# Issuing the job loads and stores of a float32 decoder layer in four parts of 256 KB

## The chip, the cores and the metric

The kernel runs on one core of one Trainium2 chip. The metric is the time of one execution on the device, in microseconds (us). The core has TensorE (PE in the profile; its weight loads are PEld), VectorE (DVE), ScalarE (ACT), GpSimd (POOL) and SyncE (SP). SP, ACT and POOL can issue DMA transfers, which are carried out by the core's 16 DMA engines. Transfers that SP issues appear as queue q1 in the profile, transfers that POOL issues as queue q0. An engine executes its instructions in a fixed order; an instruction that has to wait for a semaphore holds up everything behind it on the same engine.

## The reference

One decoder layer on 256 tokens with 2048 features, all in float32:

```
x = x + concat(pool_mixer, mla_mixer, memory_cross_attention)(rms_norm(x) @ w_in) @ w_o
h = rms_norm(x)
g = h @ w_gate                                  # 2048 x 5632
gc = conv_b + sum_j conv_w[j] * shift(g, j)     # causal, width 3
x = x + (silu(gc) * (h @ w_up)) @ w_down        # 5632 x 2048
```

The last three lines are the feed-forward block, and the change lies in its weights of `w_down`.

## The kernel before, in words

**Splitting.** TensorE multiplies rounded float32 (float32r), so each weight tile is split in two: `split_w` (lines 96 to 105) has ScalarE round a block of 1024 columns into `wh` (L102), and VectorE subtract that from the raw tile into `wl` (L103). A product is then three matmuls. In the gate and up stage `gemm_pair` (L155 to L170) does this: for each of 44 tiles f of 128 features of `w_gate` and `w_up`, 96 matmuls at L168.

**The loop over f.** The loads of the two 1 MB weight tiles come from `load_w` on SP's queue (L89), into a buffer `wr` of three; they are pinned in program order. After a step's matmuls, `glu` (L827 on) does the convolution and the gate on VectorE and ScalarE: `g` L829, `gc` L831, L833, L834, and then the product with the up half (L839 or L850). For 17 of the 22 pairs of tiles of f, `glu` also builds seven forms of the activation (L854 to L858); five pairs are written out to DRAM by POOL (L860, `forms`).

**Seven products in place of eight.** Down's weights are seen as 2 x 2 blocks of 512 columns and multiplied by a scheme of Strassen's kind that needs seven products. It needs sums of weight blocks. For 28 pairs of column half and feature pair (`SUMMED`) the sums are made ahead of time, as "jobs" beside the gate and up stage, and are kept in DRAM in `tsum`. A job loads a 1 MB tile of `w_down`, 128 partitions of 8 KB, into one of two buffers `wj` (`job_load`, L873 to L877); VectorE makes four subtractions in place, each on blocks of 512 columns (L883): block 1 from 0 and 1, block 0 from 2 and 0, block 2 from 2 and 1, block 3 from 3 and 2; then POOL stores the tile to `tsum` in two halves of 512 KB (L885). Loads, subtractions and stores are pinned (`keep`) behind what was traced before them on their engine.

**When.** The loads of jobs 0 and 1 come at the head of the loop and after step 1. `job_at` (L887) gives job i the step 1 + 37 i // 27, that is one after one or two steps of f. At that step the kernel first issues the load of job i + 1 and then the subtractions and stores of job i (L907 to L910). POOL thus has load i + 1 ahead of the stores of job i, and load i + 1 goes to the buffer of job i - 1, whose stores must have landed.

**Order.** The Tile framework traces the program, decides the order on each engine by its own simulation with its own instruction costs, and puts in the semaphores. Where `keep` pins an instruction it stays behind its predecessor in the program; the splits of `gemm_pair` are not pinned and are placed by the planner.

**Down.** After the loop, down loads raw tiles and the sums from `tsum` with SP (`load_dn`, L922 to L929), every third of them into a buffer `wj`. SP's queue takes them in the planner's order among the last loads of `w_gate` and `w_up`.

Of the kernel before, what the change touches and what calls it, by code (L numbers as in the profile page):

```python
# [37 lines left out]
HS = 1024  # L38
NN = 512
# [6 lines left out]
SUMMED = tuple((c, j) for c in range(2) for j, k in zip(ORDER, KIND) if k == "S")  # L46
# [18 lines left out]
def layer(ctx, tc, xT_d, xn_d, memT_d, vec_d, tab_d, w_z_d, w_mqkr_d, w_q_d, w_kv_d, w_mem_d, w_pool_d, w_o_d,  # L65
          w_g_d, w_u_d, w_dn_d, out_d):
    nc = tc.nc
# [18 lines left out]
    def load_w(src, n, cut=STG, kept=False):  # L86
        raw = stage.tile([P, STG], F32, tag="wr", name=nm("wr"), bufs=3)
        for c in range(0, n, cut):
            keep(nc.sync.dma_start(raw[:, c:min(n, c + cut)], src[:, c:min(n, c + cut)]), kept)  # L89
        return raw[:]  # L90

    def keep(ins, on=True):

        return tc.keep_in_program_order(ins) if on else ins
# [240 lines left out]
    for c in range(KD // 2):  # L335
        raw = raw0 if c == 0 else load_w(w_mem_d[c], STG, HS if c == 1 else STG)
# [9 lines left out]
        if c % 2:  # L346
            h = slice(2 * c - 2, 2 * c + 2)
# [68 lines left out]
    for c in range(KD // 2):  # L416
        raw = load_w(w_mqkr_d[c], 2 * 576)
# [110 lines left out]
    for m in range(6):  # L528
        raw = load_w(w_z_d[m], STG)
# [338 lines left out]
    tsum = dp.tile([P, len(SUMMED), STG], F32, name="tsum")  # L868

    def job_place():  # L870
        return fp.tile([P, STG], F32, tag="wj", name=nm("wj"), bufs=2)[:]

    def job_load(i):  # L873

        raw = job_place()
        keep(nc.gpsimd.dma_start(raw, w_dn_d[SUMMED[i]]))  # L876
        return i, raw  # L877

    def job_sums(i, raw):

        r = raw.rearrange("p (b n) -> p b n", n=NN)
        for d, a, b in ((1, 0, 1), (0, 2, 0), (2, 2, 1), (3, 3, 2)):
            keep(nc.vector.tensor_tensor(r[:, d], r[:, a], r[:, b], op=ALU.subtract))  # L883
        for h in range(2):
            keep(nc.gpsimd.dma_start(tsum[:, i, h * HS:(h + 1) * HS], raw[:, h * HS:(h + 1) * HS]))  # L885

    job_at = {1 + i * (KF - 7) // (len(SUMMED) - 1): i for i in range(len(SUMMED))}  # L887

# [8 lines left out]
    for ps, raw in zip(pss, raws):  # L897
        gemm_t(ps, raw, HS, h2, range(8, KD), first=False)
    job = job_load(0)
    for f in range(1, KF):  # L900
        rows = [load_w(w[f], STG, kept=True) for w in (w_g_d, w_u_d)]
        behind = (lambda p=pss: glu(0, *p)) if f == 1 else None
        pss = [ps_main()[:, 0:T] for _ in range(2)]
        gemm_pair(pss, rows, h2, behind)
        if f < KF - 1:
            glu(f, *pss)
        if f in job_at:  # L907
            now, n = job, job_at[f] + 1
            job = job_load(n) if n < len(SUMMED) else None
            job_sums(*now)  # L910
# [213 lines left out]
```

## Time and profile before

| what | value |
|---|---|
| time, median of 3 runs (lowest to highest) | 1006.77 us (1006.08 to 1007.03) |
| the profiled execution: its time, its span | 1005.68 us, 1003.9 us |
| TensorE / VectorE / ScalarE / POOL busy | 99% / 78% / 57% / 7% |
| job loads (L876) | 28 of 1024 KB, median 7.4 us from issue to landing |
| job stores (L885) | 56 of 512 KB, median 10.4 us from issue to landing |
| job subtractions (L883) | 112, mean 686 ns |
| the stretch of the jobs | first load at 297.5 us, last store at 733.8 us |

A row of a timeline has the start, the length, the engine and line, the operation, the tiles written and read, and in square brackets the engine's idle time ahead of it with what ended it. A row of a queue has the packets, the megabytes, and the time that they took as a share of 16 engines over the window. The row of a wait has the total, the number of times, and the longest.

### The profile page before, as it was taken

Reading aid. Unit: us, or ns where it says so; the run is one execution under the profiler, and the core shown is the slowest. Engines: PE = TensorE matmul, PEld = TensorE weight load, DVE = VectorE, ACT = ScalarE, POOL = GpSimd, SP = SyncE. Lnnn points to the kernel's source line nnn. Section 1 sums busy time; section 2 is a strip of 40 time slices with the busy share of each in tenths; the row PEclk is TensorE's granted clock in tenths of the full one; section 3 lists DMA queues with packets and bytes.
Section 4 is the critical chain, followed back from the end, with each engine's and each line's share of the span. In section 5 each row is a group of like instructions: output and inputs, shape, how many; then the busy total and the mean of one; then the engine's idle time right before and its main releaser. Section 6 shows DMA issues by size and latency. Waiting matters only on the chain.

```text
span 1003.9 us, 17322 instructions
## 1 busy us (share of the span) xinstructions
PE 992.0 (99%) x6870; PEld 917.6 (91%) x6870; DVE 785.1 (78%) x1174; ACT 570.9 (57%) x779; POOL 66.8 (7%) x130
## 2 busy tenths in 40 slices
PE   9999999999999999999999999999999999999998
PEld 8899988888899999999989999999999888888886
DVE  6877588755667887868868888788667889989987
ACT  6777666544565545435445545545445666757763
POOL 1100000000010110101011101011000000000000
PEclk9999999999999999999989999999999999999999
DMA  9867445333667988888889998999898999999992
GB/s 360 292 247 282 146 143 199 131 133 129 226 223 295 338 302 323 314 326 294 334 301 339 358 331 308 343 359 358 309 350 323 333 372 367 363 342 395 367 385 109
DMA packets 50578, 294.89 MB, mean 294 GB/s; under 512 B 5696, under 2 KB 6208, under 8 KB 25024
## 3 DMA queue, kind: packets, MB, share of 16 engines
q1 hardware_dynamic: 33696, 213.16, 57.3%
q0 software_dynamic: 16368, 79.83, 22.5%
q8 instruction: 54, 0.88, 0.3%
q10 hardware_dynamic: 432, 0.79, 0.2%
q14 instruction: 28, 0.23, 0.1%
HBM read 255.61 MB, written 38.14 MB: 293 GB/s over the span
## 4 chain that ended last, share of the span: by engine, by line
PE 84%; DMA 10%; DVE 4%; issue 1%; ACT 1%; POOL 0%; SPq 0%; DVEq 0%; POOLq 0%; ACTq 0%
PE psm L168 33%; DMA tsum<-wj 6%; PE psm L184 5%; PE psm L185 5%; PE psm L186 5%; PE psm L149 4%; PE psa L935 4%; PE psa L934 4%; PE psm L935 4%; PE psa L933 4%; PE psm L934 4%; PE psm L933 4%; PE psm L133 2%; DMA wr<-in_w_g 2%; DMA wj<-in_w_dn 2%; DVE wl L103 2%
## 5 line engine op out<-in xcount | busy, mean ns | idle before, releaser
L103 DVE TENSOR_TENSOR wl<-wr,wh 128x1024 fp32r<-128x1024 f32 (+2 forms) x344 | 396.7, 1161 | 127.8 <-ACT wh L102 119.3
L102 ACT CAST wh<-wr 128x1024 fp32r<-128x1024 f32 (+2 forms) x344 | 339.8, 1000 | 166.0 <-PE psm L185 49.1
L168 PE MATMUL psm<-h,wh 128*128 128x256 f32 x2752 | 320.9, 277 | 0.6 <-ACT wh L102 0.6
L168 PEld LDWEIGHTS psm<-h,wh 128*128 128x128 f32 x2752 | 316.9, 188 | 0.8 <-ACT wh L102 0.8
L168 PE MATMUL psm<-h,wl 128*128 128x256 f32 x1376 | 167.2, 279 | 5.9 <-DVE wl L103 5.9
L168 PEld LDWEIGHTS psm<-h,wl 128*128 128x128 f32 x1376 | 161.8, 189 | 7.4 <-DVE wl L103 7.3
L831 ACT ACTIVATE gc<-g,vec 128x256 f32<-128x256 f32 x44 | 26.5, 602 | 111.9 <-DVE g L829 111.0
L883 DVE TENSOR_TENSOR wj<-wj 128x512 f32<-128x512 f32 x112 | 76.8, 686 | 15.1 <-DMA wj<-in_w_dn 14.0
L102 ACT CAST wh<-wj 128x1024 fp32r<-128x1024 f32 (+1 forms) x48 | 47.2, 982 | 22.0 <-PE psa L934 11.6
L103 DVE TENSOR_TENSOR wl<-wj,wh 128x1024 fp32r<-128x1024 f32 (+1 forms) x48 | 53.7, 1132 | 6.0 <-ACT wh L102 2.4
L834 ACT ACTIVATE gc<-gc 128x256 f32<-128x256 f32 x44 | 18.4, 418 | 57.2 <-DVE gc L833 57.2
L833 DVE SCALAR_TENSOR_TENSOR gc<-g,vec,gc 128x255 f32<-128x255 f32 x88 | 42.2, 480 | 1.5
L103 DVE TENSOR_TENSOR wl<-dn,wh 128x1024 fp32r<-128x1024 f32 (+1 forms) x36 | 40.1, 1132 | 3.4 <-ACT wh L102 1.7
L102 ACT CAST wh<-dn 128x1024 fp32r<-128x1024 f32 (+1 forms) x36 | 35.4, 982 | 10.7 <-PE psm L934 4.9
L184 PE MATMUL psm<-wh,cat 128*128 128x512 f32 x96 | 38.1, 397 | 0.0
L186 PE MATMUL psm<-wl,cat 128*128 128x512 f32 x96 | 37.4, 390 | 0.0
L185 PE MATMUL psm<-wh,cat 128*128 128x512 f32 x96 | 37.4, 389 | 0.0
L885 POOL DMA_DIRECT2D tsum<-wj x56 | 29.8, 534 | 86.8 <-DVE wj L883 69.8
L876 POOL DMA_DIRECT2D wj<-in_w_dn x28 | 15.0, 536 | 282.3 <-DMA tsum<-wj 274.8
L934 PE MATMUL psm<-wh,aS 128*128 128x512 f32 x84 | 32.7, 389 | 0.0
L933 PE MATMUL psa<-wh,aS 128*128 128x512 f32 x84 | 32.7, 389 | 0.0
L933 PE MATMUL psm<-wh,aS 128*128 128x512 f32 x84 | 32.7, 389 | 0.0
(248 smaller groups left out, 1473.5 us busy)
## 6 DMA issues: line engine op xcount, KB each, us to landing
wr<-in_w_g SPq DMA_DIRECT2D x44, 1024.0 KB, 7.9
wr<-in_w_u SPq DMA_DIRECT2D x44, 1024.0 KB, 7.7
wj<-in_w_dn POOLq DMA_DIRECT2D x28, 1024.0 KB, 7.4
tsum<-wj POOLq DMA_DIRECT2D x56, 512.0 KB, 10.4
wr<-in_w_o SPq DMA_DIRECT2D x16, 1024.0 KB, 4.8
wr<-in_w_dn SPq DMA_DIRECT2D x16, 768.0 KB, 6.9
wr<-tsum SPq DMA_DIRECT2D x12, 1024.0 KB, 6.8
wj<-tsum SPq DMA_DIRECT2D x12, 1024.0 KB, 7.2
```

Source lines behind the costliest of these rows:

```text
L102: keep(nc.scalar.copy(hi[:, c:e], raw[:, o + c:o + e]), kept)
L103: keep(nc.vector.tensor_tensor(lo[:, c:e], raw[:, o + c:o + e], hi[:, c:e].bitcast(F32), op=ALU.subtract), kept)
L149: keep(nc.tensor.matmul(ps, parts[k // nk][low][:, i * P:(i + 1) * P], m, start=k + a == 0 and low == low_first, stop=k == KD - 1 and low ...
L168: nc.tensor.matmul(ps, parts[k // nk][low][:, i * P:(i + 1) * P], m, start=k + a == 0 and low == (s == 1), stop=k == KD - 1 and low == (s ...
L184: keep(nc.tensor.matmul(ps, xh, hi[:, i, o], start=first and i == 0, stop=False), kept)
L185: keep(nc.tensor.matmul(ps, xl, hi[:, i, o], start=False, stop=False), kept)
L186: keep(nc.tensor.matmul(ps, xh, lo[:, i, o], start=False, stop=last and i == nk - 1), kept)
L833: nc.vector.scalar_tensor_tensor(gc[:, d:T], g[:, 0:T - d], v(w, f), gc[:, d:T], op0=ALU.mult, op1=ALU.add)
L883: keep(nc.vector.tensor_tensor(r[:, d], r[:, a], r[:, b], op=ALU.subtract))
L933: nc.tensor.matmul(ps, a[0], b[0], start=first, stop=False)
L934: nc.tensor.matmul(ps, a[1], b[0], start=False, stop=False)
L935: nc.tensor.matmul(ps, a[0], b[1], start=False, stop=last)
```

## The change

The load of a job is issued as four DMAs, one for each block of 512 columns (128 rows of 2 KB each), in place of one DMA of 1 MB. The store is issued as four DMAs in place of two. The order of the calls, the subtractions and the buffers are as they were.

```
 def job_load(i):
     raw = job_place()
-    keep(nc.gpsimd.dma_start(raw, w_dn_d[SUMMED[i]]))
+    for b in range(4):
+        o = slice(b * NN, (b + 1) * NN)
+        keep(nc.gpsimd.dma_start(raw[:, o], w_dn_d[SUMMED[i]][:, o]))
     return i, raw
...
-    for h in range(2):
-        keep(nc.gpsimd.dma_start(tsum[:, i, h * HS:(h + 1) * HS], raw[:, h * HS:(h + 1) * HS]))
+    for b in range(4):
+        o = slice(b * NN, (b + 1) * NN)
+        keep(nc.gpsimd.dma_start(tsum[:, i, o], raw[:, o]))
```

NN is 512, HS is 1024.

## The prediction

> **What bounds the kernel now.** I read the page first, then TensorE's gaps in the timeline, then who waits for the tile of the jobs (wj), then the queues' packets.
>
> ```profile
> PE 992.0 (99%) x6870; PEld 917.6 (91%) x6870; DVE 785.1 (78%) x1174; ACT 570.9 (57%) x779; POOL 66.8 (7%) x130
> ```
>
> TensorE is idle for 1003.9 - 992.0 = 11.9 us, so little can be won. TensorE's timeline from 295 to 750 us, its gaps in brackets:
>
> ```profile
> 439.68 1.21 PE L168 MATMUL psm<-h,wl 128*128 128x256 f32 x8 [1.28 <-DVE wl L103]
> ...
> 441.48 1.19 PE L168 MATMUL psm<-h,wl 128*128 128x256 f32 x8 [0.58 <-DVE wl L103]
> ...
> 519.87 3.78 PE L168 MATMUL psm<-h,wl 128*128 128x256 f32 x16 [2.40 <-DVE wl L103]
> ...
> 720.48 1.19 PE L168 MATMUL psm<-h,wl 128*128 128x256 f32 x8 [0.58 <-DVE wl L103]
> ...
> 736.83 4.04 PE L168 MATMUL psm<-h,wh 128*128 128x256 f32 x32 [0.61 <-ACT wh L102]
> ```
>
> The same gaps by waits, over 302 to 785 us:
>
> ```profile
> PE psm L168 <- DVE wl L103: 5.9, 6, 2.4
> PE psm L168 <- ACT wh L102: 0.6, 1, 0.6
> ```
>
> So 6.5 us stand still in this stage. The gap of 2.40 us costs more than itself. Columns of the next view: length, busy time of each engine (instructions), then the granted clock, the DMA share and GB/s:
>
> ```profile
> 512.00:519.00 7.00, 5.47 (x46) 5.09 (x45) 5.42 (x9) 2.39 (x4) 1.59 (x3) 1.00 0.58 204
> 519.00:526.00 7.00, 6.13 (x28) 6.13 (x29) 6.14 (x9) 3.83 (x6) 0.00 (x0) 0.51 1.01 343
> 526.00:533.00 7.00, 7.00 (x64) 7.00 (x63) 5.21 (x8) 4.04 (x4) 1.06 (x2) 1.00 0.94 364
> ```
>
> Behind it the clock is 0.51 for 7 us: 28 matmuls instead of 64. The 0.87 us of gap in that window are 8 of them; the other 28, at 7.00/64 = 0.109 us, are 3.1 us. The gaps of 1.28 and 0.58 us brought no such window.
>
> What makes wl late? VectorE's timeline has these three rows just ahead of the gaps at 439, 519 and 720 us:
>
> ```profile
> 430.53 2.15 DVE L883 TENSOR_TENSOR wj<-wj 128x512 f32<-128x512 f32 x3 [3.41 <-DMA wj<-in_w_dn]
> ```
> ```profile
> 510.73 2.87 DVE L883 TENSOR_TENSOR wj<-wj 128x512 f32<-128x512 f32 x4 [4.56 <-DMA wj<-in_w_dn]
> ```
> ```profile
> 709.53 2.87 DVE L883 TENSOR_TENSOR wj<-wj 128x512 f32<-128x512 f32 x4 [4.05 <-DMA wj<-in_w_dn]
> ```
>
> The subtractions of jobs 8, 13 and 26 (counted from 0) wait for their load; the split (L103) and the gate's steps stand behind them, and TensorE starves. These three make 1.28 + 0.58 + 2.40 + 0.58 = 4.84 us of gaps, and the 3.1 us. The load is late because POOL's queue holds it. POOL's timeline, and its waits:
>
> ```profile
> 487.38 0.54 POOL L876 DMA_DIRECT2D wj<-in_w_dn  x1 [14.88 <-DMA tsum<-wj]
> 487.91 1.06 POOL L885 DMA_DIRECT2D tsum<-wj  x2
> 503.77 0.54 POOL L876 DMA_DIRECT2D wj<-in_w_dn  x1 [14.81 <-DMA tsum<-wj]
> 504.30 1.06 POOL L885 DMA_DIRECT2D tsum<-wj  x2
> ```
> ```profile
> POOL wj L876 <- DMA tsum<-wj: 274.8, 25, 15.1
> POOL tsum L885 <- DVE wj L883: 69.8, 22, 20.1
> ```
>
> With two buffers, load i+1 waits until the stores of job i-1 have landed, and the stores of job i stand behind that load. So there is a chain: stores land, load, stores, stores land. Its turns here take 503.77 - 487.38 = 16.4 us. The loop asks for 37 steps over 27 jobs (job_at) of 96 matmuls at 0.109 us, 14.3 us. The chain runs behind until a wait of POOL for VectorE (69.8 us in 22) sets it back on time.
>
> **The change part by part.** (1) Issues. POOL issues 8 DMAs per job instead of 3. A DMA with rows of 2 KB has a row: two stores of x1s. POOL's timeline and the queues between 254.5 and 258 us:
>
> ```profile
> 254.21 1.23 POOL L789 DMA_DIRECT2D x1s<-x1n  x2 [192.00 <-DVE x1n L761]
> ```
> ```profile
> q0 software_dynamic: 160, 0.52, 39.9%
> ...
> x1s<-x1n POOLq DMA_DIRECT2D x2, 256.0 KB, 2.4
> ```
>
> An issue takes 0.54 to 0.62 us, like one of 1 MB (0.54). 5 x 0.54 x 28 = 76 us on POOL, busy for 7%: hidden by its waiting of 274.8 us. Within a turn the last store is issued 3 x 0.54 + 2 x 0.53 = 2.7 us later; the load's own data, ahead of it in the queue, hide that (3.6 us, below).
>
> (2) Packets. 0.52 MB went in 128 packets of 4 KB (160 less 2 x 16 that only signal), two rows in each, at 0.399 x 16 x 3.5 / 128 = 0.174 us. For the present stores (524 to 525.6 us), the present loads (505.4 to 509.2 us) and SP's loads (529.7 to 531.2 us) the queue rows are:
>
> ```profile
> q0 software_dynamic: 169, 0.62, 95.6%
> ```
> ```profile
> q0 software_dynamic: 128, 1.00, 90.8%
> ```
> ```profile
> q1 hardware_dynamic: 79, 0.64, 100.5%
> ```
>
> A store's packet of 4 KB takes 0.956 x 16 x 1.6 / 151 = 0.162 us, the job load's of 8 KB 0.908 x 16 x 3.8 / 122 = 0.45, SP's of 8 KB 1.005 x 16 x 1.5 / 79 = 0.305. Stores: 16 packets per DMA engine and job, 0.012 more each, +0.2 us. Loads are not shown in this form: now 8 x 0.45 = 3.6 us; at best 16 x 0.174 = 2.8 (-0.8), at worst with the excess of 0.45 - 0.305 on every smaller packet 16 x 0.32 = 5.1 (+1.5). I take the present rate per byte with the 0.012 per packet, +0.2, as it is the same data from the same place. A turn of the chain grows by 0.2 + 0.2 = 0.4 us (bounds -0.6 and +1.7).
>
> While SP's loads run too, both queues take turns. The queues from 511.5 to 513.5 us:
>
> ```profile
> q1 hardware_dynamic: 67, 0.55, 64.7%
> q0 software_dynamic: 71, 0.28, 34.3%
> ```
>
> 67 packets to 71: one by one, whatever the size. Stores keep their 4 KB packets, so nothing changes for them; the load's go from 8 to 4 KB, and up to 8 more packets of SP per engine can slip in, 8 x 0.305 = 2.4 us at most, nothing where SP's queue is empty, as from 507 us on. That lies inside the upper bound of the range. The Trainium skill (DMA: Bandwidth & Descriptors, Queues, rings and completion order) has the queues alternate by packet; the trace agrees, with 67 to 71.
>
> (3) The subtractions. They need blocks 0 and 1, then 2 and 0, 2 and 1, 3 and 2. Each takes 0.70 us. Data of a quarter take 0.9 us, so against the present landing the first starts at -1.8 and the third, after block 2 at -0.9, ends at +0.5; the fourth ends at 1.2 instead of 2.87. The run ends 1.65 us earlier, less the load's 0.2: 1.45 us. That is the gain at a wait (bounds 0.15 and 2.45). Where the load had landed it is nothing.
>
> (4) The parts of a load all stand behind the same landing: a new tile in a used buffer starts when everything that used the old one is done, so no part goes ahead. If each waited for its own block's store alone, the first would start a store or two sooner; that belongs to the faster rival.
>
> (5) The end. SP's queue and ScalarE's first row there:
>
> ```profile
> 715.03 0.33 SPq L89 DMA_DIRECT2D wr<-in_w_u  x1
> 726.74 0.33 SPq L928 DMA_DIRECT2D wj<-in_w_dn  x1
> 727.16 0.78 SPq L89 DMA_DIRECT2D wr<-in_w_g  x1
> ```
> ```profile
> 735.73 2.00 ACT L102 CAST wh<-wr 128x1024 fp32r<-128x1024 f32 x2 [6.76 <-DMA wr<-in_w_g]
> ```
>
> SP waits with down's first load into wj until the stores of job 26 have landed, a load of w_g stands behind it, and that gives the gap of 0.61 us. Two turns of 0.4 later: +0.8 us, uncovered.
>
> **The sum.** Turns since the last job whose stores were held by VectorE: one for job 8, three for jobs 13 and 26. Job 8: -1.45 + 0.4 = -1.05. Jobs 13 and 26: -1.45 + 1.2 = -0.25 each; the gap of job 13 stays at 2.15 us and I leave its slow window where it is. End: +0.8. Together -0.75 us. The profiled execution took 1005.68 us (span 1003.9 and 1.8 around it), so 1004.9; the median of the runs is 1006.77, 1.09 above it: **1006.0 us**, no change that a measurement of this kernel can tell (0.2%, 2.0 us).
>
> **The rivals.** *The early start wins.* If the smaller packets read as fast as SP's (load -0.05 or better), a turn grows by 0.15 and the run ends 1.7 earlier: job 8 -1.55, job 13 -1.25 (its gap 1.15, below the 1.86 us that brought no slow window: -3.1), job 26 its whole 0.58, end +0.3: -6.2 us, 1000.6. For it: SP's 0.305 against 0.45. Against: the excess was there with SP's queue empty.
>
> *The chain takes over (slower).* Place: load and stores in POOL's queue. Break-even at job 13: 1.65 less the load's growth g equals three turns of g + 0.2, g = 0.26 us, just above what I take. At g = 0.7, jobs 13 and 26 end 3 x 0.9 - 0.95 = 1.75 later each, job 8 the same, end +1.8: +5.3 us, 1012.1. For it: turns of 16.4 us against 14.3 asked, and an end that waits for the chain. Against: POOL's 69.8 us of waiting for VectorE show that it catches up between.
>
> *Another order.* The planner places the splits among the subtractions by its own durations of these DMAs. One more gap like the one at 519 us costs 2.40 + 3.1 = 5.5 us: 1012.3. Nothing in the profile speaks for a side.
>
> *Costs per DMA that add up.* The two stores of x1s landed 2.4 us after issue, issued 0.6 us apart, so what a DMA costs beside its bytes overlaps with its neighbour's. If it did not, three more of 2.4 - 0.6 = 1.8 us would stand in each load, 5.4 us a turn, less the 69.8/27 = 2.6 us a turn that POOL waits for VectorE now: 27 x 2.8 = +76 us, 1083. The Trainium skill (DMA: Bandwidth & Descriptors, Anatomy of one DMA — SWDGE (gpsimd) path) gives a DMA of POOL 2.0 us and its bytes at 436 GB/s, by which four of 256 KB one after the other would be an estimated 10.4 us against 4.4 for one of 1 MB, and its rules for kernel authors ask for 1 MiB or more.
>
> **How the numbers follow.** No change 0.33, early start 0.31, chain 0.20, other order 0.13, costs that add up 0.03. The edges of the first case reach over by 0.04 to faster. Faster 0.35, same 0.29, slower 0.36. The range leaves out that last case and the ends: 1000.0 to 1013.5; the likeliest case alone has 1004.8 to 1008.8.
>
> **What would show it.** Step 2: POOL's queue packets of 4 KB, and how long one of a load takes (0.235 us taken; under 0.21 is the early start, over 0.27 the chain). Step 3: first subtractions of jobs 8, 13 and 26 at most a microsecond behind block 1, and smaller gaps at 439, 519 and 720 us. Step 5: SP's first wj load after 727.5 us. The clock's window of 0.51 gone, or a second one, decides more than all of these, and would make the forecast wrong.

## The result and the profile after

The changed kernel takes 1010.08 us (median of 20 runs, 1001.0 to 1014.55), the kernel before, run beside it, 1003.13 us (20 runs, 993.5 to 1011.28): a ratio of 1.0077, with a 95% interval of 1.0055 to 1.0100. It is slower, by less than one per cent but clear of the interval. The forecast was 1006.0 us, no change. 1010.08 us lies inside the range that was given with it, which took in the rivals too, but 0.75 us less than before was forecast and 6.95 us more was measured. The single runs spread over some 15 us, so the two profiled executions (1005.68 us before, 1007.68 us after) do not show the whole of the 7 us; they show at which waits the kernels differ.

The page of the kernel after: busy times, the two large DMA queues (packets, MB, share), and the DMA issues of the jobs (count, size, median from issue to landing).

```profile
PE 989.7 (98%) x6870; PEld 914.8 (91%) x6870; DVE 784.9 (78%) x1174; ACT 570.4 (57%) x779; POOL 142.3 (14%) x270
...
q1 hardware_dynamic: 33696, 213.16, 57.0%
q0 software_dynamic: 22192, 79.84, 22.9%
...
wj<-in_w_dn POOLq DMA_DIRECT2D x112, 256.0 KB, 5.8
tsum<-wj POOLq DMA_DIRECT2D x112, 256.0 KB, 9.1
```

TensorE's idle time is 1005.5 - 989.7 = 15.8 us, 3.9 more than before. POOL is busy 75.5 us longer, which is 140 more issues of 0.54 us. The waits of the kernel after over 302 to 785 us (total, times, longest):

```profile
POOL wj L878 <- DMA tsum<-wj: 262.1, 26, 14.3
POOL tsum L888 <- DVE wj L885: 26.8, 8, 16.7
DVE wj L885 <- DMA wj<-in_w_dn: 22.0, 8, 6.7
PE psm L168 <- DVE wl L103: 9.9, 8, 3.2
```

The second row is the one to read first. POOL waited 69.8 us, 22 times, for VectorE before; now 26.8 us, 8 times. So in most turns the subtractions are done when POOL comes to the stores: POOL's own chain (stores land, load, stores) is what is late. The third row is the mirror image: VectorE waits for a job's load 22.0 us (14.0 before), and the last row is what TensorE waits for VectorE's splits, 9.9 us (5.9 before). TensorE's timeline has most of it in three places, at 440, 555 and 710 us:

```profile
437.44 1.19 PE L168 MATMUL psm<-h,wl 128*128 128x256 f32 x8 [0.29 <-DVE wl L103]
...
441.06 1.30 PE L168 MATMUL psm<-h,wl 128*128 128x256 f32 x8 [2.42 <-DVE wl L103]
...
442.85 2.07 PE L168 MATMUL psm<-h,wl 128*128 128x256 f32 x8 [0.50 <-DVE wl L103]
...
555.96 1.21 PE L168 MATMUL psm<-h,wl 128*128 128x256 f32 x8 [2.38 <-DVE wl L103]
...
713.25 1.20 PE L168 MATMUL psm<-h,wl 128*128 128x256 f32 x8 [3.20 <-DVE wl L103]
```

VectorE's timeline of the kernel after, at jobs 8, 13 and 26, and then the same view of the kernel before at job 8, where the prediction showed only a part of the run:

```profile
431.68 0.69 DVE L885 TENSOR_TENSOR wj<-wj 128x512 f32<-128x512 f32 x1 [6.70 <-DMA wj<-in_w_dn]
432.64 2.15 DVE L885 TENSOR_TENSOR wj<-wj 128x512 f32<-128x512 f32 x3 [0.26 <-DMA wj<-in_w_dn]
...
510.04 2.88 DVE L885 TENSOR_TENSOR wj<-wj 128x512 f32<-128x512 f32 x4 [3.66 <-DMA wj<-in_w_dn]
...
711.37 0.69 DVE L885 TENSOR_TENSOR wj<-wj 128x512 f32<-128x512 f32 x1 [5.08 <-DMA wj<-in_w_dn]
711.98 1.22 DVE L103 TENSOR_TENSOR wl<-wr,wh 128x1024 fp32r<-128x1024 f32 x1
713.12 0.69 DVE L885 TENSOR_TENSOR wj<-wj 128x512 f32<-128x512 f32 x1
...
713.92 1.41 DVE L885 TENSOR_TENSOR wj<-wj 128x512 f32<-128x512 f32 x2
```
```profile
430.53 2.87 DVE L883 TENSOR_TENSOR wj<-wj 128x512 f32<-128x512 f32 x4 [3.41 <-DMA wj<-in_w_dn]
```

Job 8's load is issued at the same time in both (423.83 and 423.80 us). The first subtraction does not start early but 1.15 us late, and the run ends at 432.64 + 2.15 = 434.79 in place of 433.40 us, 1.39 us later. The row also shows the intended effect: the run is broken after the first subtraction, which did start before the whole load was there (the second one waits for data again). The comparison is not of the cut alone: SP issues its next weight load 0.88 us behind the job's load here (424.68 us) and 2.98 us behind it before (426.81 us), so SP's data stand beside the job's for longer.

At job 26 something else has changed too. Before, the split (L103) stands ahead of the four subtractions and does not wait for their load:

```profile
704.26 1.22 DVE L103 TENSOR_TENSOR wl<-wr,wh 128x1024 fp32r<-128x1024 f32 x1
709.53 2.87 DVE L883 TENSOR_TENSOR wj<-wj 128x512 f32<-128x512 f32 x4 [4.05 <-DMA wj<-in_w_dn]
```

In the kernel after, the planner has put this split behind the first subtraction, at 711.98 us. It now waits for the load, and TensorE's longest gap, the 3.20 us before 713.25 us, waits for it.

### The profile page after: what moved, and what is told of

Same layout as the page of the kernel before. It is cut to its first block, busy times and chain, and to the rows that moved or that the text cites. A ratio compares the mean times of both kernels' runs of the same rounds, so it can differ in the third digit from the quotient of the medians.

```text
span 1005.5 us, 17584 instructions
## 1 busy us (share of the span) xinstructions
PE 989.7 (98%) x6870; PEld 914.8 (91%) x6870; DVE 784.9 (78%) x1174; ACT 570.4 (57%) x779; POOL 142.3 (14%) x270
## 3 DMA queue, kind: packets, MB, share of 16 engines
q0 software_dynamic: 22192, 79.84, 22.9%
## 4 chain that ended last, share of the span: by engine, by line
PE 56%; DMA 26%; DVE 8%; POOL 5%; issue 4%; ACT 2%; POOLq 0%; DVEq 0%; ACTq 0%
DMA tsum<-wj 18%; PE psm L168 6%; PE psm L184 5%; PE psm L185 5%; PE psm L186 5%; DVE wl L103 4%; PE psm L149 4%; PE psa L938 4%; PE psm L938 4%; PE psa L937 4%; PE psa L936 4%; PE psm L937 4%; PE psm L936 4%; DMA wj<-in_w_dn 3%; POOL wj L878 3%
## 5 line engine op out<-in xcount | busy, mean ns | idle before, releaser
L103 DVE TENSOR_TENSOR wl<-wr,wh 128x1024 fp32r<-128x1024 f32 (+2 forms) x344 | 396.8, 1162 | 120.9 <-ACT wh L102 115.5
L878 POOL DMA_DIRECT2D wj<-in_w_dn x112 | 60.0, 541 | 271.0 <-DMA tsum<-wj 262.1
L888 POOL DMA_DIRECT2D tsum<-wj x112 | 60.4, 545 | 37.8 <-DVE wj L885 26.8
L103 DVE TENSOR_TENSOR wl<-wj,wh 128x1024 fp32r<-128x1024 f32 (+1 forms) x48 | 53.6, 1132 | 5.1 <-ACT wh L102 1.9
L103 DVE TENSOR_TENSOR wl<-dn,wh 128x1024 fp32r<-128x1024 f32 (+1 forms) x36 | 40.1, 1133 | 3.4 <-ACT wh L102 1.7
L789 POOL DMA_DIRECT2D x1s<-x1n x8 | 4.3, 545 | 223.4 <-DVE x1n L761 223.0
L937 PE MATMUL psa<-wh,aS 128*128 128x512 f32 x84 | 32.7, 389 | 0.0
L936 PE MATMUL psa<-wh,aS 128*128 128x512 f32 x84 | 32.7, 389 | 0.0
```

The source lines that it names most:

```text
L103: keep(nc.vector.tensor_tensor(lo[:, c:e], raw[:, o + c:o + e], hi[:, c:e].bitcast(F32), op=ALU.subtract), kept)
L878: keep(nc.gpsimd.dma_start(raw[:, o], w_dn_d[SUMMED[i]][:, o]))
L888: keep(nc.gpsimd.dma_start(tsum[:, i, o], raw[:, o]))
L936: nc.tensor.matmul(ps, a[0], b[0], start=first, stop=False)
L937: nc.tensor.matmul(ps, a[1], b[0], start=False, stop=False)
```

## The experiments

**Which part.** The load alone in four parts:

```
 def job_load(i):
-    keep(nc.gpsimd.dma_start(raw, w_dn_d[SUMMED[i]]))
+    for b in range(4):
+        o = slice(b * NN, (b + 1) * NN)
+        keep(nc.gpsimd.dma_start(raw[:, o], w_dn_d[SUMMED[i]][:, o]))
```

> Only the loads are in four parts; the stores stay two of 512 KB. Issue theory (a turn of POOL's chain grows because the last store is issued later, by 3 x 0.54 = 1.6 of the 2.7 us): about 1.6/2.7 of the change's +0.77%, 1.0046 of before, and the last store lands later after the first load issue by about 1 us. Packet theory (the load's packets go from 8 to 4 KB and lose to SP's loads; the stores keep their packets of 4 KB): all of it, 1.0077. Early start: below 1.000, if only the stores' part was harmful.

and the stores alone in four:

```
-    for h in range(2):
-        keep(nc.gpsimd.dma_start(tsum[:, i, h * HS:(h + 1) * HS], raw[:, h * HS:(h + 1) * HS]))
+    for b in range(4):
+        o = slice(b * NN, (b + 1) * NN)
+        keep(nc.gpsimd.dma_start(tsum[:, i, o], raw[:, o]))
```

> Only the stores are in four parts; the load stays one of 1 MB. Issue theory: 1.06 of the 2.7 us, 1.0031 of before. Packet theory: nothing, 0.999 to 1.001, since a store's packet is 4 KB in both forms.

Measured: the load 1005.4 us, ratio 1.0049 [1.0019, 1.0080]; the stores 1000.1 us, 0.9997 [0.9965, 1.0030]. The split load loses by itself, the split stores do not. The first is what the issue theory expected (1.0046), the second what the packet theory expected; neither theory has both. Whether split stores add to a split load's loss is open, as the intervals of 1.0049 and 1.0077 overlap. The waits of the first and of the second kernel:

```profile
DVE wj L885 <- DMA wj<-in_w_dn: 17.4, 8, 4.8
```
```profile
DVE wj L883 <- DMA wj<-in_w_dn: 9.7, 3, 6.6
```

VectorE waits for the load 8 times in the one, as with the whole change, and 3 times in the other (5 times, 14.0 us, in the kernel before).

**Is it the chain?** Two kernels leave the jobs' stores out, and down reads the raw weights in place of the sums; their output is not the layer's. One has the load whole, the other in four parts.

```
-    for h in range(2):
-        keep(nc.gpsimd.dma_start(tsum[:, i, h * HS:(h + 1) * HS], raw[:, h * HS:(h + 1) * HS]))
...
-            sums = load_dn(tsum[:, SUMMED.index((c, j))])
+            sums = load_dn(w_dn_d[c, j])
```

> The jobs' stores are left out, and down reads the raw weight tile in place of the sums (same bytes, so the output is not the layer's); the load is one of 1 MB. No load waits for a landing any more. Chain theory: the waits of VectorE for wj (14.0 us in before) and the gaps from them vanish, 0.990 to 0.996 of before. If the gaps come from the weights' own loads: 0.998 to 1.000.

> As the one before, with the load in four parts. Chain theory (the longer load hurts because the next stores and the next load hang on it): the same time as with one load, within 0.2%. Theory that the smaller packets or more DMAs harm the weights' loads of SP whatever the chain: 0.4% more than with one load.

Measured: 993.08 us (992.89 to 993.26) with the load whole, 993.19 us (992.96 to 993.35) with the load in four parts. The loss of the split load is gone, and so is the spread of the runs: 0.4 us in place of 15. POOL's waits of the one and of the other:

```profile
POOL wj L876 <- DVE wj L883: 317.4, 23, 25.2
```
```profile
POOL wj L878 <- DVE wj L885: 281.8, 22, 23.3
```

No load waits for a store's landing now, POOL waits for VectorE in its place: the chain "stores land, load, stores" is broken. The cut still makes the load later there: from its first issue to its whole landing it is 7.08 us with one DMA and 8.87 with four, though in both kernels the loads from job 2 on are issued within 0.6 us of the same times and SP's within 0.9. But TensorE has no gap in the jobs' stretch in either, so a slower load costs nothing there. The kernel without the chain takes some 11 us less than the kernel before (ratio 0.9886 [0.9841, 0.9932]), about what a rearrangement of the job transfers could win at most; part of it may come from the 29.4 MB that are not written there.

**Smaller rows or more DMAs?** One DMA for the load and two for the stores, but in rows of 2 KB: a gap of 64 bytes behind each block of 512 columns in the buffer keeps the rows apart, and the packets become 4 KB.

```
+        t = fp.tile([P, STG + 64], F32, tag="wj", name=nm("wj"), bufs=2)[:]
+        return t.rearrange("p (b n) -> p b n", b=4)[:, :, 0:NN] if gap else t[:, 0:STG]
...
+        keep(nc.gpsimd.dma_start(raw, w_dn_d[SUMMED[i]].rearrange("p (b n) -> p b n", n=NN)))
```

> One load and two stores per job as before, but the buffer has a gap of 64 bytes behind each block of 512 columns, so that each DMA has rows of 2 KB as in the change. Issues are those of before, packets those of the change (4 KB with two rows). Issue theory: 0.999 to 1.001. Packet theory: about 1.0077, and the job load's packets take more than half of what an 8 KB packet took.

> The kernel with one load and two stores in rows of 2 KB a second time, beside the one with idle DMAs, since its first interval (1.0012 to 1.0074) is wide. Packet theory: 1.003 to 1.007. Issue theory: 1.000.

The load in two DMAs of 512 KB, and in eight of 128 KB, with the two stores as before:

```
+        for h in range(2):
+            o = slice(h * HS, (h + 1) * HS)
+            keep(nc.gpsimd.dma_start(raw[:, o], w_dn_d[SUMMED[i]][:, o]))
```

> The load in two parts of 512 KB with rows of 4 KB (the stores as before). Packets are 4 KB, as in the change, but with one DMA more instead of three. If the packets' size makes the loss: 1.004 to 1.005, as with all the load's rows at 2 KB. If each further DMA of a load costs: about a third of the four-part load's excess, 1.001 to 1.003, with the load landed about 0.3 us later than in before.

```
+        for o in range(0, STG, NN // 2):
+            keep(nc.gpsimd.dma_start(raw[:, o:o + NN // 2], w_dn_d[SUMMED[i]][:, o:o + NN // 2]))
```

> The load alone in eight parts of 128 KB (256 columns, rows of 1 KB), the two stores as before: 10 DMAs a job, twice the cuts of the kernel whose load alone is in four parts. Theory: at each packet of POOL's queue, and at the end of each DMA, a packet of SP gets its turn, so the load lands later the more it is cut; one load had 7.4 of SP's packets per DMA engine between its issue and its landing, four parts 9.5, in eight 11 to 14, landing 1.5 to 3 us later than the 7.75 of before, ratio 1.008 to 1.020. Rival: the cut costs only until the parts no longer pass without a gap, and the last part's issue, 7 x 0.53 = 3.7 us behind the first, is covered by data: landing 7.5 to 8.7, ratio 1.000 to 1.006.

The table has, from each kernel's trace, the time from a load's first issue to the landing of all of it, and the data packets of SP's queue per DMA engine that began between the two (those of 4 bytes, which only signal, left out); both are means over the loads of jobs 2 to 27 of one execution.

| load | landed, us | SP's packets | ratio |
|---|---|---|---|
| whole (before) | 7.75 | 7.4 | 1 |
| whole, rows of 2 KB, first series | 8.04 | 7.9 | 1.0043 [1.0012, 1.0074] |
| the same, second series | 7.85 | 7.2 | 0.9984 [0.9953, 1.0016] |
| two parts | 8.05 | 7.4 | 1.0006 [0.9974, 1.0039] |
| four parts | 8.69 | 9.5 | 1.0049 [1.0019, 1.0080] |
| four parts, stores in four (the change) | 9.18 | 9.6 | 1.0077 [1.0055, 1.0100] |
| eight parts | 10.70 | 12.3 | 1.0247 [1.0207, 1.0288] |

The loss grows with the number of DMAs in a load. The smaller rows alone have 4 KB packets too, but let hardly more of SP's packets through, and their two series disagree about a loss; together they are about no change. The two series also say that half a per cent should not be read closely, the 1.0049 of the four-part load included; that a cut costs rests on the eight parts and on the waits. Eight parts lose five times what four lose, inside what the theory of SP's turns expected for the landing (1.5 to 3 us later; measured 2.95), and somewhat above its ratio; the rival, landing by 8.7 us, is out. The waits with eight parts:

```profile
DVE wj L884 <- DMA wj<-in_w_dn: 36.6, 14, 7.2
...
PE psm L168 <- DVE wl L103: 16.4, 11, 4.2
```

The growing count of SP's packets does not say by itself why a cut load is later. A load that takes longer for any reason has more of SP's packets beside it: in the two kernels without stores it is 10.5 and 13.3, which is 1.5 per us of the load's time in both. And it moves without a cut: with one store of 1 MB per job, below, the whole load has 9.0 beside it and lands after 8.1 to 8.3 us.

One load shows the shares. Queue rows of the kernel before and then of the kernel after, each from the issue of job 13's load to its landing (503.77 to 510.61 us, and 501.95 to 511.17 us):

```profile
q0 software_dynamic: 268, 1.54, 69.9%
q1 hardware_dynamic: 118, 0.84, 29.8%
```
```profile
q0 software_dynamic: 421, 1.41, 51.8%
q1 hardware_dynamic: 161, 1.18, 36.2%
```

POOL's own packets took 0.699 x 6.84 = 4.78 us before and 0.518 x 9.22 = 4.78 us after: the same. SP's took 0.298 x 6.84 = 2.04 and 0.362 x 9.22 = 3.34 us: 1.30 of the 2.38 us by which this load got longer. In 1.0 us of the rest no packet ran (1 - 0.518 - 0.362 of 9.22 us, nearly), most of it in the first 2 us. Here too the start counts: SP's load ahead of it was issued 0.12 us before the job's load, and 2.13 us before it in the kernel before, so more of SP's megabyte falls into the window. Over all the loads the 1.43 us are 0.86 of SP's packets, 0.20 of POOL's own, and 0.37 that neither queue used; without stores the 1.79 us are 0.93, 0.47 and 0.38, again with more in all three.

**POOL's time, or the DMAs?** Five idle DMAs of 1 KB beside the unchanged load and stores, three behind the load and two behind the stores:

```
+    def idle_dma(i, n):
+        for _ in range(n):
+            t = fp.tile([P, 16], F32, tag="idle", name=nm("idle"), bufs=5)
+            keep(nc.gpsimd.dma_start(t[0:16, :], w_dn_d[SUMMED[i]][0:16, 0:16]))
```

> Before, with three DMAs of 1 KB (16 rows of 64 bytes into a tile that nothing reads) behind each load and two behind each pair of stores: POOL issues eight DMAs per job as in the change, rows and packets of the real ones are those of before. Issue theory (the stores are issued later): 1.003 to 1.005. Packet theory: 0.999 to 1.001.

The same place and number, but fills of a small tile in place of DMAs:

```
+            t = fp.tile([P, 512], F32, tag="idle", name=nm("idle"), bufs=1)
+            keep(nc.gpsimd.memset(t[0:16, :], 0.0))
```

> The kernel before, and behind each job's load three fills of a small tile on POOL (16 partitions of 512 numbers, about 0.5 us each as the fill of 128x2048 took 1.825 us), behind its stores two. POOL is held as long as by five more issues (about 2.7 us a job), but no DMA is added; the fills are work that nobody reads. If it is POOL's time alone that delays the turn, this takes what the kernel with five idle DMAs took: ratio 1.004 to 1.010, and first load issue to last store about 4.2 us. If it is what a DMA costs in the queue and not its issue, ratio 0.998 to 1.002.

The three idle DMAs behind the load alone, and the two behind the stores alone, the latter profiled twice:

> The kernel before, and three idle DMAs of 1 KB behind each job's load and none behind its stores (6 DMAs a job). If what counts is how much later the stores are issued behind the load, this takes what the load alone in four parts took: ratio 1.003 to 1.008, the stores 1.6 us later. If every DMA counts the same wherever it stands, 3/5 of 1.007: 1.004, with the next kernel at 1.003.

> The kernel before, and two idle DMAs of 1 KB behind each job's stores and none behind its load (5 DMAs a job). POOL then waits for the stores to land anyway, so if only the delay of the stores counts, nothing: 0.998 to 1.002, as the stores alone in four parts. If every DMA counts the same wherever it stands: 1.003.

> One more profile of the kernel with two idle DMAs behind the stores, because its first profile was of its shortest run (1000.58 against a median of 1009.35). If the idle DMAs act on the chain of POOL, a run of about 1009 shows VectorE waiting for the jobs' loads 15 us or more (4.8 in the first profile) with loads that land in 7.2 to 7.8 us; if they act elsewhere, that wait stays under 8 us and TensorE's gaps stand at another place.

Measured: five idle DMAs 1.0070 [1.0031, 1.0109], the fills 1.0007 [0.9976, 1.0038], three behind the load 1.0070 [1.0044, 1.0097], two behind the stores 1.0074 [1.0039, 1.0110]. The fills did what the second expectation had; the five idle DMAs and the two cost more than either of theirs. From the load's issue to the last store's it is 4.43 us in the mean with the fills and 4.26 with the change (3.18 before). These means hold POOL's waits for VectorE; in the median turn it is 2.96 us with the fills, 3.85 with the change, 2.77 with the load alone in four parts and 1.29 before. So POOL's time is out as the cause of the split load's loss: with the fills the stores are issued later than with the split load, and nothing is lost. The waits with the fills:

```profile
POOL tsum L891 <- DVE wj L889: 56.7, 19, 16.9
DVE wj L889 <- DMA wj<-in_w_dn: 9.4, 3, 4.4
```

The idle DMAs do not answer for the change's parts, though they cost the same. Their loads land after 7.2 to 7.8 us, like before, and two cost as much as five, where the two more stores of the second kernel above cost nothing. The second profile of the kernel with two idle DMAs, of a run of 1009.5 us, has

```profile
DVE wj L888 <- DMA wj<-in_w_dn: 16.7, 5, 6.4
PE psm L168 <- DVE wl L103: 7.8, 6, 3.7
```

so VectorE's wait is the one expected there if they act on POOL's chain, though little above the 14.0 us of the kernel before in a run of 1005.68 us; by what step they cost time is open.

**Fewer DMAs.** One store of 1 MB per job in place of two of 512 KB; the same with the load in four parts; and the one store issued ahead of the next job's load in place of behind it.

```
-        for h in range(2):
-            keep(nc.gpsimd.dma_start(tsum[:, i, h * HS:(h + 1) * HS], raw[:, h * HS:(h + 1) * HS]))
+        keep(nc.gpsimd.dma_start(tsum[:, i], raw))
```

> Before with one store of 1 MB in rows of 8 KB in place of two of 512 KB in rows of 4 KB; the order of instructions on the other engines is that of before. Packet theory turned round: the store's packets are 8 KB and take one turn in two against SP's 8 KB, half of the bytes instead of a third, so stores land earlier (median under 10.4 us after issue) and the chain is shorter: 0.995 to 0.999. Against: the first half's store waits for all four subtractions; if that rules, 1.000 to 1.003.

> One store of 1 MB per job again (2 DMAs a job), beside the same runs of the kernel before. If fewer issues and one landing shorten the turn as its first runs had it: ratio 0.993 to 0.998. If that was chance: 0.998 to 1.002.

> The load in four parts, the store in one of 1 MB. The order on TensorE, VectorE (but for job 23), ScalarE and SP is that of before. Chain theory: the longer load costs in a shorter chain less than the 0.5% it cost with two stores: 0.997 to 1.001, and more than with one load and one store (0.9957).

```
             now, n = job, job_at[f] + 1
-            job = job_load(n) if n < len(SUMMED) else None
             job_sums(*now)
+            job = job_load(n) if n < len(SUMMED) else None
```

> Before with one store of 1 MB, and a job's store issued ahead of the next job's load instead of behind it. The store of job i no longer waits for the landing of job i-1's. Chain theory: the waits of VectorE for wj become rare, 0.990 to 0.995, down to the 993.1 us of the kernel without stores. If the load, now behind a store's 1 MB in the queue, lands too late for the next job: 0.997 or more.

One store: 999.73 us, 0.9957 [0.9925, 0.9989], and in the second series 999.46 us, 0.9989 [0.9956, 1.0023]. Its ratio is below the change's 1.0077 in both; against the kernel before, the first series says 0.4% faster and the second cannot tell. With the load in four parts 1001.12 us, 0.9984 [0.9952, 1.0015]: its loads land after 9.43 us, and it is still no slower than before. Turns in which the stores stand directly behind the load (issued within 0.5 us of it) take 14.75 us there, 15.46 with the change, 14.90 before, 13.59 and 13.10 with one store and the load whole. So the load's landing alone does not decide. That the turn of the chain does is argued from these numbers, not shown: with the stores alone in four parts it is 15.02 us, and nothing is lost. Stores ahead of the load: 1044.34 us, 1.0416 [1.0382, 1.0449].

```profile
POOL tsum L884 <- DVE wj L883: 395.5, 27, 23.3
DVE wj L883 <- DMA wj<-in_w_dn: 71.7, 15, 7.9
```

There POOL waits for VectorE with the next load behind the wait, and VectorE then waits 71.7 us for loads. The planner put VectorE's instructions in another order throughout the stage in this kernel, so the 4% are not the stores' place alone.

**Cut by partitions.** Four loads of 32 partitions with whole rows of 8 KB, four stores of 64 partitions with rows of 4 KB: as many DMAs as with the change, larger packets.

```
+        for q in range(4):
+            p = slice(q * 32, (q + 1) * 32)
+            keep(nc.gpsimd.dma_start(raw[p], w_dn_d[SUMMED[i]][p]))
```

> Eight DMAs per job as in the change, but cut by partitions: loads as 4 x 32 partitions of 8 KB rows, stores as 2 halves x 2 groups of 64 partitions of 4 KB rows. Packets are those of before, the number of issues that of the change; no subtraction can start before the whole load. Issue theory: 1.008 or a little over. Packet theory: 0.999 to 1.001.

1042.81 us, 1.0418 [1.0377, 1.0459], but it decides nothing, as the planner put the splits of the whole stage in another order. Its queue row is of use below.

## Why the prediction was wrong, point by point

**The step that failed is (2), the load's time on the queue.** The sum took +0.2 us for a load, with bounds of -0.8 and +1.5; measured is +1.43, at the upper bound. The term has two parts, and a third was missing. POOL's own packets were priced by the rate per byte with 0.012 us more per packet: +0.2, measured +0.20. The turns of SP's queue were named ("up to 8 more packets of SP per engine can slip in, 2.4 us at most") and then entered at nothing, with the reason that SP's queue is empty where job 13's load runs. In the mean over the loads it is not: 9.6 of SP's packets in place of 7.4, 0.86 us. The remaining 0.37 us, in which neither queue used the engines, had no term in the sum. And the rule was not the one argued. By packets alone the kernel with 2 KB rows should have let in as many; it did not. Counted by DMAs, about 0.7 of SP's packets come in for each additional one of the load: (9.5 - 7.4) / 3 = 0.7 with four parts, (12.3 - 7.4) / 7 = 0.7 with eight, none with two. That it is the end of a DMA at which SP gets its turn is a guess from these counts; as a longer load has more of SP's packets beside it in any case, why the cut load is later stays open. The Trainium skill (DMA: Bandwidth & Descriptors, The descriptor swizzle) has one completion descriptor per side and engine behind the data of a transfer of 1 MiB to 128 partitions; the traces agree in so far as the change's 140 more DMAs add 2240 packets under 512 B, 16 for each.

The sign that the prediction set for this step, how long one of a load's 4 KB packets takes, shows nothing of this: it is some 0.22 us (the first 256 data packets of POOL's queue from 1 us behind the issue), near the 0.235 taken and under the 0.27 that was to show the chain. Most of the load's growth stands beside POOL's packets, not in them.

With the measured growth of the load, 1.43, and of a turn, 0.56 (below), in place of 0.2 and 0.4, the prediction's own sum gives 0.34 us for job 8, 1.46 each for jobs 13 and 26, and 1.1 for the end: an estimate of +4.4 us in place of -0.75, most of the 6.95.

**(1) The issues: right.** POOL's 75.5 us more are hidden, and so are the later stores: the fills, which hold POOL nearly as long (71.3 us more), cost nothing (1.0007).

**(3) The early start: right in kind, eaten.** The first half of a load lands 6.10 us after its issue in place of 7.75, 1.65 us earlier, but the run of subtractions needs all four blocks, and 1.65 less the load's 1.43 leaves little. At job 8 the prediction had the end of the run 1.05 us earlier, and it is 1.39 later; at job 13, counted from the load's issue, it ends after 512.92 - 501.95 = 10.97 us in place of 513.60 - 503.77 = 9.83.

**The rival "The chain takes over" is the nearest to what happened.** Its point of decision was a load growth of 0.26 us; it was priced at 0.7 and got 1.43. It had 0.20 of the chance. Its price per turn was too high: the turn did not grow by the load's growth and 0.2 more, 1.6 us, but by 0.56 us (14.90 to 15.46 where the stores stand directly behind the load; the sum's own 0.4 was near), since the stores, whose data follow in the same queue, land 0.74 us sooner after their first issue (12.32 in place of 13.06 over all turns). There are more such turns, though, 22 in place of 15, and so the lateness adds up: job 26's load is issued at 704.04 us in place of 697.45. The end of the chain is as this rival had it:

```profile
728.54 0.33 SPq L931 DMA_DIRECT2D wj<-in_w_dn  x1
```

SP's first load into wj comes at 728.54 us, 1.8 us later; step (5) had +0.8, the rival +1.8. Its time of +5.3 us is near the 6.95 of the medians, but so are the +5.5 of "Another order"; the time alone does not tell them apart.

**The other rivals.** "The early start wins" is out with the load's landing. "Another order" came in part. In the stage, the instructions of TensorE, ScalarE and SP stand in the same order, but VectorE's differ at one place, and it is job 26, where TensorE's longest gap of the kernel after stands (3.20 us, 0.58 behind this job before). The order alone does not make the loss: every kernel here with the load cut by columns has it, and with two parts, or with four and one store, the time is that of before (1.0006 and 0.9984), while the loss grows from two parts to eight in the same order of VectorE. At that place the four-part load alone has a gap of 0.24 us, and the two just named have none. So the order makes a late load dear at job 26; what it adds to the 0.8% is not known, as no run has the split load in the old order. (The expectation of the kernel with a split load and one store names this place as job 23; the subtractions at 709.53 us are job 26's.) "Costs per DMA that add up" is out in its size: a further DMA in a load costs 0.3 us (four parts alone, 0.94 / 3) to 0.5 us (the change, 1.43 / 3), not 1.8. Its estimate from the Trainium skill's price per DMA (DMA: Bandwidth & Descriptors, Anatomy of one DMA — SWDGE (gpsimd) path), 10.4 us in place of 4.4, is far from the 9.18 in place of 7.75 measured. The Trainium skill's rule of 1 MiB or more per DMA (DMA: Bandwidth & Descriptors, Rules for kernel authors) has the right side: the one store of 1 MB is faster than two of half the size in one series (0.9957) and not to be told from them in the other (0.9989).

**The clock.** The prediction left the slow window at 519 us where it was. The kernel after has it elsewhere, and a milder one (columns as in the prediction's windows):

```profile
438.00:445.00 7.00, 4.08 (x24) 3.59 (x23) 5.49 (x8) 4.79 (x6) 2.87 (x6) 0.78 0.95 304
445.00:452.00 7.00, 7.00 (x61) 7.00 (x61) 4.79 (x9) 3.27 (x4) 0.00 (x0) 0.97 1.02 424
...
711.00:718.00 7.00, 4.75 (x41) 4.75 (x42) 6.59 (x10) 0.60 (x1) 1.91 (x4) 1.00 0.96 360
718.00:725.00 7.00, 7.00 (x64) 7.00 (x63) 4.40 (x9) 4.34 (x6) 2.38 (x5) 1.00 0.88 291
```

That is also why the profiled execution lost 2.0 us while TensorE's idle time grew by 3.9: its busy time, which the slow windows stretch, fell by 2.3.

## What to carry to other kernels

Where a transfer waits for an earlier one and shares its DMA engines with another busy queue, price a cut of it by more than its own bytes and issues: here it cost some 0.3 to 0.5 us for each further DMA in a load of 1 MB, of which its own packets were a small part. An early start on the first quarter was worth little to a run of subtractions that needs the last quarter soon after. Look first at who waits for whom on the issuing queue: in the kernels without stores POOL waits for VectorE, and there the same cut costs nothing. And compare the order of the instructions wherever the changed kernel waits longest: a change of DMAs alone moved a split behind the subtraction that waits.

## What the runs showed that was not expected

Idle DMAs of 1 KB cost 0.7%, whether two, three or five per job and on whichever side of the stores, while POOL's time for as many costs nothing; the reason was not found. Two further real stores, in the same place as two of the idle DMAs, cost nothing.

Cutting loads and stores by partitions made their bytes slower. The queue row of that kernel (span 1040.6 us) has POOL's queue busy for 0.254 x 1040.6 = 264 us, against 0.229 x 1005.5 = 230 us after, for the same 79.84 MB:

```profile
q0 software_dynamic: 18608, 79.84, 25.4%
```

A gap of 3.20 us of TensorE left the granted clock at 1.00 in the 7 us behind it, while 2.42 us, with gaps of 0.29 ahead and 0.50 behind, was followed by 0.78. The length of the gap alone does not say whether the clock falls. In the clock records of the two traces the slow stretch of the jobs' stage lasts 6.83 us before and 3.41 us after, and begins a whole number of 3.41 us behind the start of the fast clock (150 times before, 128 times after). On this grid the gap of 2.42 us lies within one step and the gap of 3.20 us across two. The Trainium skill (TensorE: Matmul & The Clock Gate, Part 1: The HAM clock gate) has the clock halved after an idle window of about 3.4 us that runs freely; the grid agrees with such a window, but the falls here came behind gaps shorter than it, so a window idle in full is not what these runs show as the condition.

The spread of the kernel before, 993.5 to 1011.28 us, goes with the jobs' stores: without them the runs agree within 0.4 us.
